# Softmax weights of three head pairs turned as 32x32 squares by VectorE and SBUF copies, in place of TensorE transposes

## The chip, the cores and the metric

The kernel runs on one core of one Trainium2 chip. The metric is the device time of one execution in microseconds (us), lower is better; for the kernel before it is the median of three runs. All durations below come from one profiled execution of that kernel.

## What is computed

One layer of a bidirectional encoder on 512 positions of width 1024 in float32: a recurrent branch and an attention branch side by side, an output projection, a squared-ReLU MLP, norms between. The change is in the attention branch, and in the order of the steps around it:

```
h = RMSNorm(x);  xr, gate, q, k, v = split(h @ W_in)
y_rnn  = (scan_fwd(conv(xr)) + scan_bwd(conv(xr))) * gelu(gate)
y_attn = 8 heads of 64: three windows of dilated keys (128,1),(512,4),(2048,16),
         relative bias, the three outputs combined by their softmax denominators
x = x + concat(RMSNorm(y_rnn), RMSNorm(y_attn)) @ W_out
x = x + relu(RMSNorm(x) @ W_up)^2 @ W_down;  out = RMSNorm(x)
```

The combination of the three windows equals one softmax over the union of the keys, with the logarithm of how often a key occurs added to its logit. The kernel computes it so: one matrix of weights for each head, already with the bias.

## The kernel before

Positions are sorted by parity, so that the 512 positions are four blocks of 128: two of even and two of odd ones. Every matrix product that matters is made of three passes in the fast float format (high times high, high times low, low times high parts, `mm3`); ScalarE makes the high part of a weight (`conv_hi`, tile `whi`), VectorE the low part (`conv_lo`, tile `wlo`), three chunks ahead of TensorE.

The attention stage is one written-out loop, which sets the order on all engines (nothing is reordered): steps `i` = 0..4 and, in each, `u` = 0..3. The heads go in four pairs `p`. A step (i, u) with i < 4 works on pair i and on one block of 128 queries; block numbers follow `QSEQ` = 0, 3, 1, 2. It holds:

- `att_s` (u = 0 and 2, for two u at once): 12 products q times k into `ps`, four PSUM buffers.
- `att_e`: for each of the two heads VectorE adds the bias table `tw` to `ps` and takes the minimum (tile `e`, 128 queries by 416 keys), and ScalarE takes the exponential in place and sums it into `zs`.
- `att_t` and `att_c` (i >= 1, for pair i-1, whose queries are all done): the weights have queries on partitions; the product with `v` wants keys there. For each block of 128 keys and each head, TensorE transposes three 128x128 blocks through PSUM (tile `pt`), ScalarE copies them to `ett`, and VectorE turns the fourth block, of which only 32 columns are used, itself.
- `att_av`: product of `ett` with `v` into `pav`, 12 products for a pair (each is two instructions, as float32 matmuls are in the trace), then VectorE multiplies by `zrow`, the reciprocals of the sums (tile `yp`), and ScalarE squares (`ysq`) and scales it (`at`). Pair 0 is done at (2, 2), before `att_s`; pairs 1 and 2 at (4, 0); pair 3 after the loop.
- `att_z`, `att_zd`: the sums go out to memory (`zd`) at u = 0, and come back spread over the partitions (`zrow`) at u = 2, through SP's queue.
- `load_tw`: four loads of the bias tables at u = 0 and at u = 2, through SP's queue too.
- `fill`: one to four pieces of independent work (`pqk`: projections of the next pairs' q and k; `pwo`: output projection of the recurrent branch), each one `mm3` of three passes, so that TensorE has work while the other engines do the softmax. `FILL` gives their number.
- `beside`: small steps of the recurrent branch, splits of q and k (`s_hi`, `s_lo`), and so on, by the table `plan`.

VectorE, ScalarE and TensorE each take their instructions strictly in this order. SP issues nearly all loads, also in order, and an issue that waits holds up those behind it. Tiles of one 128x512 size come from a ring of 45 (`g_`). Names in the trace: `ps` logits, `e` weights, `ett` turned weights, `pav` product with v, `nbd` bias table in memory, `kk` key parts, `hs` and `ga` recurrent state, `wraw` weights as loaded.

Of the kernel before, what the change touches and what calls it, by code (L numbers as in the profile page):

```python
# [12 lines left out]
FT = mybir.dt.float32  # L13
# [85 lines left out]
def hybrid_kernel(ctx: ExitStack, tc, xw0, xw, xn, w_in, w_v, w_out, w_up, w_dn, gates, vecs, bias, fg, out):  # L99
# [228 lines left out]
    xwt, w3 = [], []  # L328
# [18 lines left out]
    def cvx(k):  # L347
        x, w = xwt[k][:, :S], xwt[k][:, S if k else XG:]
        g = ag[:, k:k + 1] if k else xwt[0][:, S:S + 1]
        hi, lo = g_("w3h", FR), g_("w3l", FR)  # L350
# [143 lines left out]
    def conv_a(t, pp):  # L494
        xr = g_("xr")
        nc.vector.tensor_tensor(in_turn(xr), by_parity(pp), by_parity(rstd), op=OP.mult)
        c = g_("xc")
        act(c, xr, AF.Identity, scale=vec("w2", t), bias=vec("cb", t))
        xrt[t], xc[t] = xr, c

    def conv_b(t):
        xr, c = xrt.pop(t), xc[t]
        stt(c[:, 2:], xr[:, :S - 2], vec("w0", t), c[:, 2:], op0=OP.mult, op1=OP.add)
        stt(c[:, 1:], xr[:, :S - 1], vec("w1", t), c[:, 1:], op0=OP.mult, op1=OP.add)
        stt(c[:, :S - 1], xr[:, 1:], vec("w3", t), c[:, :S - 1], op0=OP.mult, op1=OP.add)
        xcs[t] = swapped("xcs", c)
# [3 lines left out]
    xcs = {}  # L510

    def swapped(name, t):
        o = g_(name)
        for b in range(2):
            nc.sync.dma_start(o[halves[1 - b]], t[halves[b]])
        return o
# [23 lines left out]
    lru_a, lru_t = {}, {}  # L540

    def lru_exp(t):
        for d in range(2):
            r = gact[t, 2 * d]
            a = g_("la")
# [11 lines left out]
    def scan_ops(t):  # L557
# [27 lines left out]
        def keep_hs():  # L585
            r1()
            hs[1] = swapped("hs", hs[1])
            scanned[t] = hs
# [219 lines left out]
    def att_e(p, u):  # L808
# [8 lines left out]
        for e in range(2):  # L817
            h = 2 * p + e
            t = g_("e")
# [9 lines left out]


# [6 lines left out]
    def att_t(h, jt):  # L837
# [5 lines left out]
        t = et[h, jt] = g_("ett")  # L843
# [88 lines left out]

    def att_av(p, jts):
        if 0 in jts:
            pav[p] = ps_("pav", "gs" if p else "pj")
        for jt in jts:
# [193 lines left out]
    for key, fs in (((4, 1, 2), [(att_a, 2), (o_sum, "s1", 0), (o_sum, "s2", 0), (o_sum, "s3", 0), (o_sum, "s3", 1), (o_sum, "22", 0)]),  # L1130
                    ((4, 2, 0), [(o_hi, "s2", 0), (o_hi, "11", 0)]), ((4, 2, 2), [(o_lo, "s2", 0), (o_lo, "11", 0)]),
                    ((4, 3, 0), [(att_q, 2), (o_hi, "11", 1), (o_hi, "s3", 0), (o_hi, "s3", 1)]), ((4, 3, 2), [(o_lo, "11", 1), (o_lo, "s3", 0)]),
                    ((4, 3, 4), [(att_y, 2), (o_lo, "s3", 1), (o_hi2, 0), (o_hi, "s1", 0), (o_hi, "22", 0)])):
        plan[key] = [op(*a) for a in fs]
# [3 lines left out]
    AVS = {(2, 2): (0,), (4, 0): (1, 2)}  # L1138
    with tc.manual_schedule(engines={nc.sync.engine}):
        for i in range(5):  # L1140
            for u in range(4):
                if i < 4:
                    if i == 2 and u == 2:
                        att_av(0, range(4))
                    if u % 2 == 0:
                        att_s(i, (u, u + 1))
                    if u == 2 and i < 3 or u == 0 and i:
                        for e in range(2):
                            load_tw(2 * (i + u // 2) + e, u // 2)
                if i >= 1:  # L1150
# [4 lines left out]
                if i >= 1:  # L1155
# [4 lines left out]
                for p in AVS.get((i, u), ()) if i == 4 else ():  # L1160
                    att_av(p, range(4))
# [4 lines left out]
                if u == (1 if i == 4 else 2) and i >= 1:  # L1166
                    att_zd(i - 1)
# [6 lines left out]
                fill(FILL.get((i, u), (1, 1, 1, 1))[3])  # L1174
                add_x()
# [24 lines left out]
    def wo_x(w, tt):  # L1200
# [3 lines left out]
        if w in ("s4", "21", "s1", "22"):  # L1204
            x1n[g, n] = g_("x1n")
# [75 lines left out]
    rb, opa, opsplit, opdone = {}, {}, {}, set()  # L1281
# [4 lines left out]
    def up_pair(q):  # L1286
# [5 lines left out]
        for n in ("s1", "s2", "s3", "22"):  # L1292
            opa[n, p] = g_("as")
# [64 lines left out]
    def h_hi(n, m):  # L1358
        hsp[n, m] = (g_("hh", FR), g_("hl", FR))
# [155 lines left out]
    for half in range(2):  # L1515
        c0, cd = cu.get((half, 0)), cd_[half]
        rb_done.clear()
        opdone.clear()
        seq = chunks[cd:cd + 7 * NQ]
# [290 lines left out]
```

## Time and profile before

| | |
|---|---|
| median of 3 runs | 525.26 us (525.24 to 526.14) |
| span of the profiled execution | 524.0 us |
| mean DMA rate over the span | 201 GB/s |
| HBM read and written | 95.59 MB and 4.29 MB |
| attention loop, from the first `ps` to the end of the second `pav` group | 94.0 to 165.25 us |

The page gives no other time of the profiled execution than its span. The difference between 525.26 and 524.0 is the start and end that the span leaves out, and the spread of runs.

How to read it: PE is TensorE (PEld its weight loads), DVE VectorE, ACT ScalarE, POOL GpSimd, SP SyncE, SPq and POOLq the DMA queues that they issue to. A row of the timeline is start, duration, engine, line, operation, out<-in with partitions x elements, and in brackets the idle time before it with what ended it. Instructions of one engine overlap a little, so that the distance from start to start is less than a duration. The chain of waits lists the work that ended last, each piece with the time in which nothing else could have ended the program sooner.

### The profile page before, as it was taken

How to read it: one execution, taken by the hardware profiler on the slowest of the kernel's cores; microseconds unless marked ns; L12 is line 12 of the kernel's file. 1: busy time of each engine (PE TensorE's matmuls, PEld its weight loads, DVE VectorE, ACT ScalarE, POOL GpSimd, SP SyncE). 2: the span in 40 equal slices, each digit the busy share in tenths (PEclk: the TensorE clock that was granted, in tenths of full speed). 3: DMA queues.
4: the chain of work that ended last, by engine and by line, in shares of the span. 5: the costliest groups of instructions: out<-in, count | busy, mean ns of one | idle time of the engine just before them, and what ended most of it. 6: DMA issues, size and time to landing. Idle time of an engine off the chain costs nothing.

```text
span 524.0 us, 8211 instructions
## 1 busy us (share of the span) xinstructions
PE 517.3 (99%) x3021; PEld 444.0 (85%) x3021; DVE 430.3 (82%) x668; ACT 351.9 (67%) x568; POOL 65.8 (13%) x90
## 2 busy tenths in 40 slices
PE   9999999999999999999999999999999999999995
PEld 8867888778787788899999888889999999888884
DVE  6899986788886898898789987789766978986985
ACT  7579946667855848585578666565667577655664
POOL 0173000000000321001300311001101300140000
PEclk9999999999999999999999999999999999999999
DMA  8636545367696499847595899976977497799804
GB/s 288 213 98 198 160 155 180 91 182 206 185 286 218 102 194 275 326 129 196 136 225 144 217 273 275 309 268 161 295 235 194 116 226 208 154 286 256 201 1 161
DMA packets 40329, 105.15 MB, mean 201 GB/s; under 512 B 5056, under 2 KB 13376, under 8 KB 40288
## 3 DMA queue, kind: packets, MB, share of 16 engines
q1 hardware_dynamic: 32448, 78.10, 44.7%
q0 software_dynamic: 7696, 26.32, 27.1%
q8 instruction: 24, 0.39, 0.3%
q10 hardware_dynamic: 144, 0.20, 0.1%
q14 instruction: 17, 0.14, 0.1%
HBM read 95.59 MB, written 4.29 MB: 191 GB/s over the span
## 4 chain that ended last, share of the span: by engine, by line
PE 96%; issue 2%; DVE 1%; POOL 1%; DVEq 0%; ACT 0%; POOLq 0%; ACTq 0%
PE pu L313 10%; PE pu L312 10%; PE pu L314 10%; PE pd L312 10%; PE pd L313 10%; PE pd L314 10%; PE pqk L312 3%; PE pqk L314 3%; PE pqk L313 3%; PE pwo L312 2%; PE pt L842 2%; PE pwo L314 2%; PE pwo L313 2%; PE ps L806 2%; PE pav L942 2%
## 5 line engine op out<-in xcount | busy, mean ns | idle before, releaser
L269 DVE TENSOR_TENSOR wlo<-wraw,whi 128x1024 fp32r<-128x1024 f32 x71 | 86.6, 1221 | 23.1 <-ACT whi L247 22.9
L247 ACT ACTIVATE whi<-wraw 128x1024 fp32r<-128x1024 f32 x67 | 70.8, 1058 | 37.5 <-PE pd L314 18.2
L313 PE MATMUL pd<-wlo,ah 128*128 128x512 f32 (+1 forms) x195 | 75.2, 386 | 0.0
L312 PE MATMUL pd<-whi,ah 128*128 128x512 f32 (+1 forms) x195 | 75.2, 386 | 0.0
L314 PE MATMUL pd<-whi,al 128*128 128x512 f32 (+1 forms) x195 | 75.2, 386 | 0.0
L314 PE MATMUL pu<-hh,wlo 128*128 128x256 f32 x224 | 63.4, 283 | 0.0
L313 PE MATMUL pu<-hl,whi 128*128 128x256 f32 x224 | 63.4, 283 | 0.0
L312 PE MATMUL pu<-hh,whi 128*128 128x256 f32 x224 | 63.4, 283 | 0.0
L269 DVE TENSOR_TENSOR wlo<-tw,whi 128x1024 fp32r<-128x1024 f32 x37 | 45.2, 1221 | 18.1 <-ACT whi L247 18.1
L312 PE MATMUL pu<-h2h,whi 128*128 128x256 f32 (+1 forms) x200 | 60.1, 300 | 0.0
L313 PE MATMUL pu<-h2l,whi 128*128 128x256 f32 (+1 forms) x200 | 60.0, 300 | 0.0
L314 PE MATMUL pu<-h2h,wlo 128*128 128x256 f32 (+1 forms) x200 | 60.0, 300 | 0.0
L247 ACT ACTIVATE whi<-tw 128x1024 fp32r<-128x1024 f32 x38 | 40.1, 1059 | 26.3 <-PE pd L314 6.3
L247 ACT ACTIVATE whi<-ts 128x1024 fp32r<-128x1024 f32 x24 | 25.5, 1061 | 26.3 <-PE pd L314 18.3
L312 PEld LDWEIGHTS pu<-hh,whi 128*128 128x128 f32 x224 | 43.0, 192 | 0.0
L313 PEld LDWEIGHTS pu<-hl,whi 128*128 128x128 f32 x224 | 43.0, 192 | 0.0
L314 PEld LDWEIGHTS pu<-hh,wlo 128*128 128x128 f32 x224 | 43.0, 192 | 0.0
L314 PEld LDWEIGHTS pd<-whi,al 128*128 128x128 f32 x195 | 36.6, 188 | 7.4
L312 PEld LDWEIGHTS pd<-whi,ah 128*128 128x128 f32 x195 | 36.6, 188 | 7.3
L313 PEld LDWEIGHTS pd<-wlo,ah 128*128 128x128 f32 x195 | 36.6, 188 | 7.3
L312 PEld LDWEIGHTS pu<-h2h,whi 128*128 128x128 f32 x200 | 38.3, 191 | 1.3
L314 PEld LDWEIGHTS pu<-h2h,wlo 128*128 128x128 f32 x200 | 38.3, 191 | 1.3
(277 smaller groups left out, 1219.8 us busy)
## 6 DMA issues: line engine op xcount, KB each, us to landing
wraw<-in_w_up_dram SPq DMA_DIRECT2D x25, 512.0 KB, 4.4
ts<-in_w_dn_dram POOLq DMA_DIRECT2D x24, 512.0 KB, 13.3
wraw<-in_w_dn_dram SPq DMA_DIRECT2D x24, 512.0 KB, 9.2
tw<-in_w_up_dram SPq DMA_DIRECT2D x15, 512.0 KB, 5.1
tw<-in_w_up_dram POOLq DMA_DIRECT2D x15, 512.0 KB, 8.3
wraw<-in_w_in_dram SPq DMA_DIRECT2D x13, 512.0 KB, 3.8
ts<-in_w_dn_dram SPq DMA_DIRECT2D x8, 512.0 KB, 6.8
tw<-in_w_dn_dram SPq DMA_DIRECT2D x8, 512.0 KB, 7.3
```

What stands on the lines that cost most here:

```text
L247: act(hi, raws[i], AF.Copy)
L269: nc.vector.tensor_tensor(lo, r, f(splits[i][0]), op=OP.subtract)
L312: nc.tensor.matmul(o, lhsT=a[0], rhs=b[0], start=bool(first), stop=False, skip_group_check=on)
L313: nc.tensor.matmul(o, lhsT=a[0], rhs=b[1], start=False, stop=False, skip_group_check=on)
L314: nc.tensor.matmul(o, lhsT=a[1], rhs=b[0], start=False, stop=bool(last), skip_group_check=on)
L806: nc.tensor.matmul(psq[p, u][e][:, :NK], lhsT=qs_[p, a][r, P * qt:P * qt + P], rhs=kks[p][r, b, w:w + NK], start=i == 0, stop=i == 2)
L842: nc.tensor.transpose(pt[:, i * P:(i + 1) * P], en[h][qt][:, k:k + P], ident)
L942: nc.tensor.matmul(pav[p][a, co], lhsT=vs[:, jt, h * DH:(h + 1) * DH], rhs=et[h, jt][:, ci], start=jt == 0 and i == 0, stop=jt == 3 and i ...
```

## The change

For pairs 0, 1 and 2 the turning leaves TensorE and ScalarE. The weights of the two heads of one query block now stand side by side in a tile of 1024 columns (`ez`, two of them, whose unused columns are zero). VectorE turns such a tile in 32x32 squares with one instruction of 128x1024 (`att_d`, tile `turn`, four for a pair). Each 32x32 square is then right in itself, but the squares of a column must still change partitions: 16 copies inside SBUF of 32 partitions by 4 KB each (`att_m`, 128 KB each, 2.1 MB a pair) bring group i of 32 partitions to place j, 11 through SP's queue and 5 through POOL's. `att_av` then reads runs of 32 or 64 columns (`ev_parts`): three products instead of one or two for a key block, with the same sum of 416 columns. It comes at (1, 2), (2, 2) and (3, 2) for pairs 0, 1 and 2, behind `att_s` and ahead of `att_e`. `zrow` is fetched at u = 1. Pair 3 keeps the old way. The ring of 45 tiles becomes a ring of 25, two boxes of eight tiles, two twins of two and one of three; the output projection's steps in `plan` come one or two u earlier.

```diff
-    NG = 45
+    NG = 25
+    def box(name, dt=FT):
+        return work.tile([P, 8, S], dt, name=name, tag="g8", bufs=2)
+    def twin(name):
+        return work.tile([P, 2, S], FT, name=name, tag="g2", bufs=2)
...
     def att_e(p, u):
-            t = g_("e")
+            t = ez[far][:, e, :] if p < 3 or u < 2 else g_("e")
...
+    ez = [twin("e") for _ in range(2)]
+    POS = (0, 2, 3, 1)
+    def att_d(p, u):
+        if u == 0:
+            turn[p] = box("turn")
+        qt = QSEQ[u]
+        nc.vector.transpose(at_(turn[p], P // 4 * POS[qt], [P, 8], [1024, 4], [1, 32]), ez[QT[qt][1]])
+    def att_m(p):
+        t, b = turn.pop(p), box("ett")
+        t, b = [x.rearrange("p (a c) n -> p a (c n)", c=2) for x in (t, b)]
+        for i in range(4):
+            for j in range(4):
+                (nc.gpsimd if 4 * i + j in (3, 6, 9, 12, 15) else nc.sync).dma_start(b[32 * j:32 * j + 32, i, :], t[32 * i:32 * i + 32, j, :])
+        eb[p] = b
...
+    def ev_parts(p, e, jt):
...
+            if jt not in qs:
+                yield at_(b, c, [1024, 4], [1, 64]), at_(o, P * qs[0], [32, 4], [d, 2], [1, 32])
+            else:
+                a0 = 3 * h0
+                yield at_(b, c + 1024 * a0, [1, 64]), at_(o, P * qs[0] + 32 * a0, [d, 2], [1, 32])
+                k = 1 - qs.index(jt)
+                a1 = 1 - h0
+                yield at_(b, c + 1024 * a1 + 32 * k, [1024, 3], [1, 32]), at_(o, P * qs[k] + 32 * a1, [1, 96])
...
-    AVS = {(2, 2): (0,), (4, 0): (1, 2)}
+    AVS = {(1, 2): (0,), (2, 2): (1,), (3, 2): (2,)}
...
-                    if i == 2 and u == 2:
-                        att_av(0, range(4))
                     if u % 2 == 0:
                         att_s(i, (u, u + 1))
+                    for p in AVS.get((i, u), ()):
+                        att_av(p, range(4))
...
-                if i >= 1:
+                if i == 4:
                     att_t(2 * i - 2, u)
                     att_t(2 * i - 1, u)
...
-                if u == (1 if i == 4 else 2) and i >= 1:
+                if u == 1 and i >= 1:
                     att_zd(i - 1)
...
+                if i < 3 and u:
+                    for v in {1: (0, 1), 2: (2,), 3: (3,)}[u]:
+                        att_d(i, v)
+                    if u == 3:
+                        att_m(i)
                 add_x()
```

On TensorE, at step (1, 2), before:

```order
L806 MATMUL ps<-kk,qh 128x416 x8
L806 MATMUL ps<-kk,ql 128x416 x4
L842 MATMUL pt<-ident,e 128x128 x6
L312 MATMUL pqk<-h_hi,whi 128x512
L313 MATMUL pqk<-h_lo,whi 128x512
L314 MATMUL pqk<-h_hi,wlo 128x512
```

and now, the first rows at the same place (shapes are those of the output; nine more rows of `pav` follow, then `pqk`):

```order
L817 MATMUL ps<-kk,qh 128x416 x8
L817 MATMUL ps<-kk,ql 128x416 x4
L992 MATMUL pav<-ett,vs 64x2x32 x2
L992 MATMUL pav<-ett,vs 64x96 x2
L992 MATMUL pav<-ett,vs 64x4x2x32 x4
```

The six transposes are gone, and the product of pair 0 with v, which stood one i later, comes directly behind the logits of pair 1.

On VectorE, from the end of step (1, 1) to the middle of (1, 2), before (`ISA e,mn` and `ISA mn` are the two instructions of the bias sum with its minimum, for one head):

```order
L269 TENSOR_TENSOR wlo<-wraw,whi 128x1024
L615 TENSOR_TENSOR ysq<-ysq 128x512
L822 ISA e,mn<-ps,tw 128x416
L822 ISA mn 128x1
L822 ISA e,mn<-ps,tw 128x416
L822 ISA mn 128x1
L851 STREAM_TRANSPOSE ett<-e 128x32 x2
L765 TENSOR_TENSOR kraw<-pqk,rrow 128x512
```

and now:

```order
L275 TENSOR_TENSOR wlo<-wraw,whi 128x1024
L855 STREAM_TRANSPOSE turn<-e 128x8x4x32 x2
L626 TENSOR_TENSOR ysq<-ysq 128x512
L1007 TENSOR_TENSOR yp<-pav,zrow 128x512
L833 ISA e,mn<-ps,tw 128x416
L833 ISA mn 128x1
L833 ISA e,mn<-ps,tw 128x416
L833 ISA mn 128x1
L776 TENSOR_TENSOR kraw<-pqk,rrow 128x512
L855 STREAM_TRANSPOSE turn<-e 128x8x4x32
```

Two large transposes of pair 1 stand ahead of `yp` of pair 0, which itself stands ahead of the logits of (1, 2); a third follows.

On SP's queue, from the end of step i = 0 into i = 1, before:

```order
L785 DMA kk<-kk 128x2x256
L230 DMA wraw<-in_w_out_dram 128x1024
L476 DMA tw<-nbd 128x384
L478 DMA tw<-nbd 128x2x160
L476 DMA tw<-nbd 128x384
L478 DMA tw<-nbd 128x2x160
L874 DMA zd<-zt 4x32x32
L230 DMA wraw<-in_w_out_dram 128x1024
```

and now:

```order
L796 DMA kk<-kk 128x2x256
L236 DMA wraw<-in_w_out_dram 128x1024
L862 DMA ett<-turn 32x1024 x11
L484 DMA tw<-nbd 128x384
L486 DMA tw<-nbd 128x2x160
L484 DMA tw<-nbd 128x384
L486 DMA tw<-nbd 128x2x160
L910 DMA zd<-zt 4x32x32
L915 DMA zrow<-zd 64x1x512 x2
L236 DMA wraw<-in_w_out_dram 128x1024
```

Eleven of the sixteen copies stand ahead of the bias tables, `zd` and `zrow`; the latter have moved from u = 2 to u = 1.

More of the change, by code (lines that the diff above doesn't have):

```diff
@@ L1204, in wo_x @@
         if w in ("s4", "21", "s1", "22"):
-            x1n[g, n] = g_("x1n")
+            if n == 0 and tt == 0:
+                st["x1n"] = twin("x1n")
+            if w == "s1" and tt == 0:
+                st["x1k"] = work.tile([P, 3, S], FT, name="x1n", tag="kk", bufs=1)
+            x1n[g, n] = st["x1n"][:, tt, :] if n == 0 else g_("x1n") if g == 1 else st["x1k"][:, g and g - 1, :]
         stt(x1n.get((g, n), x1[g, n]), po[b][tt], (nrc if n else rc[1])[:, g:g + 1], x1[g, n], op0=OP.mult, op1=OP.add)
@@ L1291, in up_pair @@
             q = p + HF // 4
-        for n in ("s1", "s2", "s3", "22"):
-            opa[n, p] = g_("as")
+        if not opb:
+            opb.append(box("as"))
+        for n, m in enumerate(("s1", "s2", "s3", "22")):
+            opa[m, p] = opb[0][:, 4 * n + p, :] if n < 2 else g_("as")
         a11, a21, a12, a22 = rb[p, 0], rb.pop((p, 1)), rb[q, 0], rb[q, 1]
@@ L1518, in hybrid_kernel @@
         opdone.clear()
+        opb.clear()
         seq = chunks[cd:cd + 7 * NQ]
```

69 lines of the change are left out of this document (48 added, 21 removed).

## The prediction

> **What bounds the kernel now.** I read the page first: the busy shares, then the chain of work that ended last.
>
> ```profile
> span 524.0 us, 8211 instructions
> PE 517.3 (99%) x3021; PEld 444.0 (85%) x3021; DVE 430.3 (82%) x668; ACT 351.9 (67%) x568; POOL 65.8 (13%) x90
> ...
> PE 96%; issue 2%; DVE 1%; POOL 1%; DVEq 0%; ACT 0%; POOLq 0%; ACTq 0%
> ```
>
> TensorE is busy for 99% of the span and is 96% of the chain, so anything taken off TensorE counts, as long as nothing else becomes late. Next come the busy times by step of the attention loop (rows: i = 0, 1, 2, 3).
>
> ```profile
> 94.00:108.00 14.00, 14.00 (x73) 10.94 (x72) 12.04 (x27) 9.57 (x22) 0.00 (x0) 1.00 0.47 129
> 108.00:124.60 16.60, 16.60 (x97) 13.39 (x96) 12.43 (x37) 12.35 (x30) 0.00 (x0) 1.00 0.64 190
> 124.60:144.20 19.60, 19.60 (x123) 15.01 (x122) 17.50 (x47) 15.20 (x35) 1.04 (x1) 1.00 0.67 184
> 144.20:159.50 15.30, 15.30 (x96) 12.47 (x97) 11.61 (x33) 10.08 (x26) 0.00 (x0) 1.00 0.96 298
> ```
>
> The columns are length, busy PE, PEld, DVE, ACT, POOL, granted clock (1.00 in all four rows), DMA share and GB/s. PE is full in each. VectorE has only 1.96, 4.17 and 2.1 us left in i = 0, 1, 2, and to these the change gives more work.
>
> **What goes from TensorE.** The chain of waits, in order of time, prices a group of six transposes (`pt`), with and without it:
>
> ```profile
> 94.07 1.33 PE ps L806 x12
> 95.40 0.43 PE pqk L312
> ...
> 108.11 1.33 PE ps L806 x12
> 109.44 0.80 PE pt L842 x6
> 110.24 0.23 PE pqk L312
> ...
> 112.75 0.23 PE pqk L314
> 112.98 0.66 PE pt L842 x6
> 113.64 0.23 PE pqk L312
> ...
> 116.41 1.32 PE ps L806 x12
> ...
> 158.83 0.66 PE pt L842 x6
> 159.49 5.76 PE pav L942 x48
> 165.25 0.43 PE pwo L312
> ```
>
> At odd u a group costs 0.66. Behind `ps` it costs 0.80 + 0.23 - 0.43 = 0.60. Twelve groups go: 6 x 0.66 + 6 x 0.60 = **7.56 us**. ScalarE loses 24 copies to `ett`, which nothing waits for once the transposes are gone; I give that nothing.
>
> The product with v keeps its columns, but has 48 instructions a pair where it had 24.
>
> ```profile
> L942 PE MATMUL pav<-ett,vs x96: 299/379/563, 132.9 to 174.0; 128*64 128x416 f32 x32, 128*64 128x256 f32 x32, 128*64 128x160 f32 x32
> 132.93 3.02 PE L942 MATMUL pav<-ett,vs 128*64 128x416 f32 x24
> 136.28 0.68 DVE L948 TENSOR_TENSOR yp<-pav,zrow 128x512 f32<-128x512 f32 x1
> ```
>
> From 160 to 256 columns a duration grows by 80 ns, 0.83 ns a column. The 24 instructions of a pair hold 24 x 277 columns, 5.5 us one after another; the group took 3.02, so the two heads run side by side and columns fill 2.77 of it. Bounds for twice the instructions: 0, or another 3.0 a pair. I take 0.2, since the remainder beyond the columns is 0.25. From the group's start to `yp` are 3.35 us, 3.55 with this.
>
> **What comes to VectorE.** Rows of its timeline in i = 0, and two tile rows of transposes:
>
> ```profile
> 101.15 1.22 DVE L269 TENSOR_TENSOR wlo<-wraw,whi 128x1024 fp32r<-128x1024 f32 x1
> 102.28 0.58 DVE L822 CUSTOM_DVE_ANT_0 e<-ps,tw 128x416 f32<-128x416 f32 x1
> ...
> 104.04 0.69 DVE L765 TENSOR_TENSOR kraw<-pqk,rrow 128x512 f32<-128x512 f32 x1 [0.65 <-PE pqk L314]
> ...
> 105.25 0.58 DVE L822 CUSTOM_DVE_ANT_0 e<-ps,tw 128x416 f32<-128x416 f32 x1
> ...
> 106.27 0.69 DVE L784 TENSOR_TENSOR kk<-kraw,kk 128x512 fp32r<-128x512 f32 x1
> 106.87 1.22 DVE L269 TENSOR_TENSOR wlo<-wraw,whi 128x1024 fp32r<-128x1024 f32 x1
> ...
> L440 DVE STREAM_TRANSPOSE cst<-ysq x2: 702/708/714, 130.2 to 177.6; 128x512 f32<-128x512 f32 x2
> L851 DVE STREAM_TRANSPOSE ett<-e x32: 168/188/208, 110.3 to 170.9; 128x32 f32<-128x32 f32 x32
> ```
>
> Start to start, a pair of logits takes 1.02, a 128x512 operation 0.60, a `wlo` 1.13. Transposes of 32 and 512 columns take 0.188 and 0.708, so 1024 columns make 1.26, or 1.17 start to start. Four a pair are **4.7 us**. In i = 0 the old work ends at 106.87 + 1.13 = 108.00; add 4.7, less the 0.65 of waiting that fills up: the last transpose of pair 0 ends at 112.05. The split `kk` moves from 106.27 to about 109.1 and ends near 109.7, while `att_s` wants it at 108.4: TensorE loses 1.15 there. It reaches the product with v at 116.41 - 1.26 + 1.15 + 1.33 = 117.6, so the copies have 5.5 us.
>
> **What the copies take.** The nearest copies inside SBUF are `xcs`, 128 KB over 64 partitions; then two stretches (the first while two such copies ran, the second with the fastest loads):
>
> ```profile
> L515 SPq DMA_DIRECT2D xcs<-xc x8: 461/568/588, 29.5 to 38.5; - x8
> ...
> DMA to landing us min/median/max: 2.2/2.2/2.4
> ...
> 30.70:31.30 0.60, 0.60 (x4) 0.49 (x3) 0.59 (x1) 0.60 (x2) 0.52 (x2) 1.00 0.95 205
> ...
> 151.00:159.00 8.00, 8.00 (x50) 6.60 (x49) 4.81 (x16) 5.35 (x14) 0.00 (x0) 1.00 0.97 337
> ```
>
> The first lands 2.2 us after its issue. Each further 131 KB takes 0.64 at 205 GB/s, 0.39 at 337, with the DMA engines 95 and 97% busy. Sixteen land 2.2 + 15 x 0.64 = 11.8, or 2.2 + 15 x 0.39 = 8.0 us after the last transpose; issue at 0.57 each on SP is no slower. I take the middle, **9.9**, because part of the time the two queues serve different halves of the partitions.
>
> [...]
>
> **The cycle.** The added wait stands ahead of all TensorE work of (1, 2); behind it `yp`, and in VectorE's order `yp` stands ahead of the next logits, hence of the next pair's transposes. So: last transpose, copies 9.9, product to `yp` 3.55, then VectorE to its next last transpose. For that stretch ScalarE counts too:
>
> ```profile
> 137.05 0.63 ACT L609 ACTIVATE ysq<-yp 128x512 f32<-128x512 f32 x1 [1.79 <-DVE yp L948]
> 137.59 0.71 ACT L962 ACTIVATE at<-yp,vt 128x512 f32<-128x512 f32 x1
> ...
> 138.95 0.64 ACT L823 ACTIVATE e<-e,mn 128x416 f32<-128x416 f32 x1
> ...
> 140.24 0.64 ACT L778 ACTIVATE kk<-kraw 128x512 fp32r<-128x512 f32 x1
> ```
>
> `ysq` 0.54, `at` 0.62, two exponentials 1.29. In i = 1 the third transpose starts 0.77 + 0.54 + 0.62 + 1.29 = 3.2 to 3.3 after `yp`; then 1.17, logits 1.02, `kk` 0.6, a `ysq` that waits for ScalarE till 7.1, 0.6, `wlo` 1.13, transpose 1.17: 10.0. In i = 2: 3.5 + 1.17 + 1.02 + 0.6 + 1.13 + 0.66 + 1.17 = 9.25.
>
> Product of pair 0 at 112.05 + 9.9 = 121.95. Second last transpose 121.95 + 3.55 + 10.0 = 135.5, product of pair 1 at 145.4. Third 145.4 + 3.55 + 9.25 = 158.2, product of pair 2 at 168.1. Then the product itself 3.15 and seven pieces of `pwo` at 0.69, to 176.1; the last exponentials of pair 3 come at about 177.1 (behind `yp` 0.6, two pairs of logits, 0.66 and 1.13, then 1.0 on ScalarE), and the six `pt` end at 177.75. Before, this point was 165.25. So **+12.5 us**: 7.56 saved, and some 20 of new waiting (4.4 at pair 0, about 6 each at pairs 1 and 2, the rest at `kk`, `pt` and the 0.6 of the products). Behind this point the program is the same. The smaller ring and the new boxes I give nothing: the number of tiles is the same, and the one box that waits (`turn`, for the copies of the pair before) is free at 121.95, ahead of `yp`. POOL is idle there but for one 1.04 us instruction.
>
> The span gives 524.0 + 12.5 = 536.5. The median of the runs shown lies 525.26 - 524.0 = 1.26 above the span: **537.8 us**. With 8.0 and 11.8 for the copies, three times -1.9 and +1.9: 532.1 to 543.5.
>
> **Rivals.**
> - *Faster: the copies hide.* If they land within the 5.5 us that TensorE leaves and a transpose of 1024 columns takes 0.5 us or less, so that four fit in the 2 us that VectorE has free, only the gain stays: 525.3 - 7.56 + 0.6 = 518.3. For it: PE is the chain. Against it: 0.708 already for 512 columns, and 2.2 for one copy. Chance 0.15; within 0.2%, between this and the next, 0.05.
> - *VectorE alone sets the pace.* The copies hide, but from one last transpose to `yp` VectorE has, in i = 1, two pairs of logits 2.04, `rz` and `zt` 0.65, six 128x512 operations 3.8, `wlo` 1.13, two transposes 2.34 and `ysq` 0.6, together 10.6, then the 10.0; in i = 2, with the two `yl` and the column sums in place of four of the six, 11.8 and 9.25: last transposes at 112.05, 132.7, 153.7, the third product at 159.2, 168.8 instead of 165.25: 528.8. Chance 0.17.
> - *`zrow` is later than the product.* SP issues it behind eleven copies and four tables, and only once `zd` has landed.
>
> ```profile
> L879 SPq DMA_DIRECT2D zrow<-zd x8: 536/586/876, 120.3 to 165.2; - x8
> ...
> DMA to landing us min/median/max: 3.1/4.9/6.0
> ```
>
>   If the queue is strictly in order, four tables 2.6 behind 9.9, `zd` 0.5, the second issue 0.6 and 3.1 make 16.7 against 13.45: 3.3 for each of pairs 0 and 1, and up to 7.5 for pair 2, behind `ws` and `x`: 544 to 552. No landing of `zd` is in the trace, so I take 0 in the sum and keep this for the range. Chance 0.18.
> - *32 partitions carry half of what 64 do*: 1.28 a copy, 21.4 for sixteen, 572. Chance 0.03. [...]
>
> **How the numbers follow.** Forecast 0.42, `zrow` 0.18, VectorE alone 0.17, hidden 0.15, same 0.05, half rate 0.03. The range 525 to 552 leaves out the hidden case, the half rate and part of the same. About 0.2% is what a measurement of this kernel can tell from no change. Faster 0.15, same 0.05, slower 0.80.
>
> **What would show it.** `pt` x24; TensorE idle ahead of three `pav` groups, with a DMA as releaser, some 4 to 6 us each; a transpose near 1.26 us; `turn` copies landing some 10 us after the last transpose; `yp` 3.5 us behind the start of `pav` (later, if `zrow` rules). No idle ahead of `pav`, or transposes near 0.6, would prove me wrong.

## The result and the profile after

The changed kernel takes 562.36 us (median of four runs, 560.72 to 562.56), the kernel before 525.48 in the same session (525.24 to 526.14): a ratio of 1.069, 95% interval 1.0673 to 1.0707, slower by 37 us. The forecast was 537.8 with a range of 525 to 552: the sign was right, the time lies above the range.

From the page of the changed kernel: span, busy time by engine, and the chain that ended last by engine.

```profile
span 558.7 us, 8300 instructions
PE 523.2 (94%) x3021; PEld 444.8 (80%) x3021; DVE 441.6 (79%) x656; ACT 342.8 (61%) x544; POOL 73.7 (13%) x107
...
PE 60%; DVE 3%; SPq 2%; issue 2%; DMA 2%; POOL 1%; ACT 0%; DVEq 0%; ACTq 0%; POOLq 0%
```

TensorE was busy 99% and is now 94%. Its busy time did not fall by the 7.6 us of the saved transposes; it rose by 6. The same stretches as before the prediction (length, busy PE, PEld, DVE, ACT, POOL, granted clock, DMA share, GB/s):

```profile
94.00:108.00 14.00, 14.00 (x74) 10.90 (x73) 12.81 (x25) 8.21 (x18) 0.00 (x0) 1.00 0.43 127
108.00:124.60 16.60, 10.41 (x60) 7.64 (x60) 12.51 (x25) 6.18 (x15) 2.50 (x5) 0.91 0.76 193
124.60:144.20 19.60, 18.06 (x100) 13.11 (x96) 13.39 (x28) 8.44 (x19) 2.42 (x5) 0.90 0.56 159
144.20:159.50 15.30, 9.16 (x69) 6.72 (x70) 8.09 (x18) 4.16 (x8) 1.05 (x1) 0.78 0.74 187
```

TensorE is no longer full from 108 on, and the granted clock, 1.00 in all four rows before, falls as far as 0.78. VectorE is not full either. The loss is waiting. Here is where: TensorE's timeline at the three products with v (start, duration, instruction, in brackets the idle time ahead of it and what ended it).

```profile
123.10 5.77 PE L992 MATMUL pav<-ett,vs 128*64 128x64 f32 x48 [5.41 <-DMA ett<-turn]
152.00 5.01 PE L992 MATMUL pav<-ett,vs 128*64 128x64 f32 x48 [3.46 <-DMA ett<-turn]
180.39 6.04 PE L992 MATMUL pav<-ett,vs 128*64 128x64 f32 x48 [6.03 <-DMA ett<-turn]
```

And VectorE's timeline at the first transposes of the next pair and at `yp`:

```profile
123.48 2.37 DVE L855 STREAM_TRANSPOSE turn<-e 128x1024 f32<-128x1024 f32 x2 [3.86 <-DMA ett<-turn]
130.70 0.69 DVE L1007 TENSOR_TENSOR yp<-pav,zrow 128x512 f32<-128x512 f32 x1 [4.27 <-DMA zrow<-zd]
...
159.51 0.69 DVE L1007 TENSOR_TENSOR yp<-pav,zrow 128x512 f32<-128x512 f32 x1 [4.23 <-DMA zrow<-zd]
...
190.62 0.69 DVE L1007 TENSOR_TENSOR yp<-pav,zrow 128x512 f32<-128x512 f32 x1 [7.46 <-DMA zrow<-zd]
```

Three things stand out. The idle time ahead of each product, 3.5 to 6 us, is what the prediction expected. The product itself takes 5 to 6 us and not 3.15. And `yp` waits for `zrow`, not for the product. Two windows (columns as above) show the first product and the copies ahead of it:

```profile
112.00:123.00 11.00, 5.69 (x32) 4.31 (x30) 7.50 (x17) 4.82 (x11) 2.50 (x5) 0.94 0.91 239
123.10:128.40 5.30, 5.30 (x46) 4.12 (x48) 2.94 (x3) 0.00 (x0) 0.00 (x0) 0.50 0.58 126
```

While the copies run, the DMA engines are 91% busy at 239 GB/s; the product then runs at a granted clock of 0.50 (the second, 152.00 to 157.01, at 0.62; the third, 180.39 to 186.43, at 0.50). SP's own timeline over the same stretch shows why `zrow` is late:

```profile
111.92 9.15 SPq L862 DMA_DIRECT2D ett<-turn  x11
121.11 0.58 SPq L484 DMA_DIRECT2D tw<-nbd  x1
121.73 0.45 SPq L486 DMA_DIRECT2D tw<-nbd  x1
122.23 0.47 SPq L484 DMA_DIRECT2D tw<-nbd  x1
122.74 0.43 SPq L486 DMA_DIRECT2D tw<-nbd  x1
123.27 0.67 SPq L910 DMA_DIRECT2D zd<-zt  x1
127.50 1.23 SPq L915 DMA_DIRECT2D zrow<-zd  x2
```

`zt` was ready at 113.64 (VectorE's timeline has it from 113.43 for 0.21), but SP issues in order: eleven copies, four tables, then `zd` at 123.27. SP then stands still until `zd` has landed (127.50) and only then issues `zrow`: three such waits, 10.8 us in all, 3.9 the longest.

The chain from the first last transpose to the common point after pair 2, beside the prediction's terms. The measured columns are differences of starts in the trace (last transposes end at 111.90, 140.62 and 169.23; the first `pt` group of the last pair ends at 197.61).

| term | predicted | measured, pairs 0, 1, 2 | later by |
|---|---|---|---|
| end of the first last transpose | 112.05 | 111.90 | -0.15 |
| last transpose to start of product | 9.9 | 11.20, 11.38, 11.16 | 4.04 |
| start of product to `yp` | 3.55 | 7.60, 7.51, 10.23 | 14.69 |
| `yp` to next last transpose | 10.0, 9.25 | 9.92, 9.72 | 0.39 |
| third `yp` to end of the first `pt` group | 6.10 | 6.99 | 0.89 |
| behind that point | 358.75 | 361.09 | 2.34 |

The sum is 22.2, which is 558.7 less the forecast span of 536.5. (The median lies 24.6 over its forecast: the profiled execution, 560.72, was the fastest of the four, and it took 2.0 more than its span where 1.26 had been added.)

Of the 14.69, the product alone accounts for 6.2: it ended 5.8, 5.0 and 6.0 after its start, where `yp` had been forecast for 3.55. The other 8.5 are `zrow`, which came 1.8, 2.5 and 4.2 after the product's end.

### The profile page after: what moved, and what is told of

It is laid out like the page before. It is cut to its first block, busy times and chain, and to the rows that moved or that the text cites. A ratio compares the mean times of both kernels' runs of the same rounds, so it can differ in the third digit from the quotient of the medians.

```text
span 558.7 us, 8300 instructions
## 1 busy us (share of the span) xinstructions
PE 523.2 (94%) x3021; PEld 444.8 (80%) x3021; DVE 441.6 (79%) x656; ACT 342.8 (61%) x544; POOL 73.7 (13%) x107
## 4 chain that ended last, share of the span: by engine, by line
PE 60%; DVE 3%; SPq 2%; issue 2%; DMA 2%; POOL 1%; ACT 0%; DVEq 0%; ACTq 0%; POOLq 0%
PE pu L320 10%; PE pu L319 10%; PE pu L318 10%; PE pd L319 9%; PE pd L318 9%; PE pd L320 9%; SPq L862 1%; DMA zd<-zt 1%; PE pwo L318 1%; PE pwo L320 1%; PE pwo L319 1%; PE pxt L1283 1%; DMA zrow<-zd 1%; POOL wlo L265 0%; DVE e L833 0%
## 5 line engine op out<-in xcount | busy, mean ns | idle before, releaser
L834 ACT ACTIVATE e<-e,mn 128x416 f32<-128x416 f32 x32 | 20.3, 635 | 38.1 <-DVE mn L833 38.1
L319 PEld LDWEIGHTS pu<-h2l,whi 128*128 128x128 f32 x200 | 38.3, 191 | 1.3
```

Of the source, the lines that this page charges most:

```text
L319: nc.tensor.matmul(o, lhsT=a[0], rhs=b[1], start=False, stop=False, skip_group_check=on)
L834: act(x, x, AF.Exp, scale=-1.0, bias=mn, accum_out=zs[p][:, 4 * e + qt:4 * e + qt + 1])
```

## The experiments

All ratios are against the kernel before, run beside each kernel (its medians lie between 525.3 and 525.9). Starting points are the changed kernel (562.36) or an experiment named.

**Whether the copies are the loss.** They are left out, once for all pairs and once for pairs 1 and 2; the products then read the turned tile as it is, with its blocks not exchanged.

```diff
     def att_m(p):
+        eb[p] = turn.pop(p)
+        return
```

> The 48 copies are left out, and the products read the turned tiles in place, so their blocks are not exchanged and what the attention branch gives is another thing; the VectorE transposes stay, with all else. Theory (the copies, and the wait for zrow that they put off, are the loss): TensorE does not idle ahead of the products, the clock stays at 1.0 and the products take 3.1 us; what is left is VectorE's added work, less the transposes saved on TensorE: 523 to 533. Rival (VectorE's transposes are most of the loss): 545 or more.

`e4_nocopy` measured: 533.89 us, 1.0159 (1.0144 to 1.0174): 28.5 us of the 37 go with the copies, and with most of the wait for `zrow`, which they put off. The products took 3.07 each, with no idle time ahead; only the third `yp` still waited, 4.67 for `zrow`.

> Copies for pair 0 alone; the products of pairs 1 and 2 read the turned tiles in place (blocks not exchanged there). Theory (each pair's copies lengthen the way from one last transpose to the next, here by 28.7 - 20.8 = 7.9 us): some 8 us more than e4_nocopy, 540 to 543. Rival (the loss comes from pair 2 alone, where the copies meet the loads of ws and x): 533 to 535.

`e17_pair0` measured: 542.85 us, 1.0322 (1.0295 to 1.0348): 9.0 more than without copies, and three times that is 27. So pair 0 pays about a third of the 28.5, and the last pair alone is not the loss; how pairs 1 and 2 divide the other 19.5 is not shown.

**What is left without copies.** As without copies, and `yp` multiplies by `rstd`, a row that is long there.

```diff
-            nc.vector.tensor_tensor(y[:, ::-1], pav.pop(p), zrow.pop(p), op=OP.mult)
+            z = zrow.pop(p)
+            nc.vector.tensor_tensor(y[:, ::-1], pav.pop(p), z if p == 3 else rstd, op=OP.mult)
```

> The copies are left out as in e4_nocopy, and yp of pairs 0 to 2 multiplies by a row that is long there in place of zrow, so the weights' sums are left out too; zd and zrow are still transferred, in the old order, and nothing waits for them. Theory (VectorE's own work, with nothing waited for, is the floor of this change): yp of pair 2 no longer waits its 4.7 us, and unlike e6_nocopy_zq and e11_nocopy_order no table comes later for it: 528 to 531, slower than before the change all the same. Rival (the floor lies under the kernel before, and order and waits alone made it slow): 518 to 524.

`e14_nocopy_noz` measured: 532.07 us, 1.0126 (1.011 to 1.0143), 1 us over the expected stretch. VectorE's timeline, second and third last transpose:

```profile
131.51 1.24 DVE L855 STREAM_TRANSPOSE turn<-e 128x1024 f32<-128x1024 f32 x1
...
153.35 1.23 DVE L855 STREAM_TRANSPOSE turn<-e 128x1024 f32<-128x1024 f32 x1
```

They end at 132.75 and 154.58; the rival "VectorE alone sets the pace" had 132.7 and 153.7. So that rival was worked out well. With neither copies nor `zrow` waited for, the change is still 6.2 us slower than the kernel before in the same session, although one of its products took 4.04, where the first took 3.08.

Two other ways to get there, with `zd` and `zrow` issued elsewhere, went the other way:

> The 48 copies are left out and the products read the turned tiles in place (blocks not exchanged, another attention result), and zd and zrow of pairs 0 to 2 go out on the POOL queue. Left of the change are VectorE's transposes and the transposes saved on TensorE. Theory (VectorE's own work is then the only thing that sets the pace): the 4.7 us that the third yp waited for zrow in the run without copies go, and the end comes 3 to 5 us earlier: 529 to 531. Rival (TensorE, no longer waiting for copies, sets the pace, and the gain on it shows): 518 to 522. Rival (zrow did not matter once the copies are gone): 534.

`e6_nocopy_zq` measured: 540.13 us, 1.0277: slower than with `zrow` in its old place. VectorE's timeline, third `yp`:

```profile
170.63 0.69 DVE L1009 TENSOR_TENSOR yp<-pav,zrow 128x512 f32<-128x512 f32 x1 [7.67 <-DMA zrow<-zd]
```

The expectation missed that SP's standing still for `zd` also held back tables and weights. On POOL's queue `zd` no longer holds them back: for pair 2 SP issued `ws`, four tables and six loads of `x` between 155.02 and 162.12, `zd` went out among them at 159.33, and `zrow` could be issued only at 167.27, 7.9 us later. Without copies and with `zd` on SP (`e4_nocopy`) that step took 2.5.

> The copies left out as in e4_nocopy (products read the turned tiles in place), and zd and zrow ahead of the tables on SP. Theory (with copies and zrow out of the way VectorE's own work sets the pace, last transposes some 21 us apart; e6_nocopy_zq failed to show it because its tables, no longer held back behind SP's wait for zd, landed ahead of zrow): yp of pair 2 no longer waits its 4.7 us, 528 to 531. Rival (something else, such as the pt groups or the ScalarE copies of the last pair, sets the end): 533 to 534 as in e4_nocopy.

`e11_nocopy_order` measured: 537.68 us, 1.0235. Here `zrow` came in time and the tables late instead:

```profile
166.11 0.59 DVE L833 CUSTOM_DVE_ANT_0 e<-ps,tw 128x416 f32<-128x416 f32 x1 [2.14 <-DMA tw<-nbd]
```

**Moving one wait at a time, with all copies.**

```diff
-        nc.sync.dma_start(bass.AP(tensor=zd.tensor, offset=zd.offset + 32 * P * p, ap=[[32, 4], [P, 32], [1, 32]]), zt)
+        (nc.sync if p == 3 else nc.gpsimd).dma_start(bass.AP(tensor=zd.tensor, offset=zd.offset + 32 * P * p, ap=[[32, 4], [P, 32], [1, 32]]), zt)
```

(and the same for the two `zrow` transfers)

> zd and the two zrow transfers of pairs 0 to 2 go out on the POOL queue, right behind its five copies, and not on SP behind eleven copies and four tables; nothing else is moved. Theory (two things end side by side ahead of each yp, the product at half clock and, a little later, zrow): yp then waits for the product only, 128.9, 157.0 and 186.4 in the trace of the changed kernel where zrow came at 130.6, 159.4 and 190.5, so 1.7 + 2.4 + 4.1 = 8.2 us go: 554. Rival (zrow alone sets the pace): the whole idle time ahead of the three yp goes, 4.3 + 4.2 + 7.5 = 16 us: 546. Rival (VectorE's own work sets the pace, the waits are slack): no change, 562.

`e1_zq` measured: 555.56 us, 1.056 (1.0542 to 1.0577): 6.8 less, near the theory's 8.2. `yp` is now released by the product, but the copies took 13.7, 13.3 and 11.7 where they had taken 11.2. That the number came so near the theory is partly luck: in the two traces the third `yp` is only 3.4 us earlier (187.20 against 190.62), and the spans differ by 2.6; the rest of the 6.8 lies between executions, and no trace shows it.

> Nothing is left out and no queue is changed; on SP zd goes out behind the fifth copy (zt is ready by then) and the two zrow behind the eleventh, ahead of the four tables, where both stood behind the tables. Theory (what makes zrow late is the tables' bytes ahead of zd on the DMA engines and SP's wait for zd; not the queue as such): zrow lands before the product ends, so yp waits for the product alone, and the copies keep their 11 us, where e1_zq, which let tables and weights start earlier, stretched them to 13.5. That is 1.7 + 2.4 + 4.1 us less than the changed kernel: 552 to 555, and up to 3 us less if the later tables also help the copies. Rival (zd and zrow, wherever issued, land behind all that is under way): yp still waits for zrow, 560 to 563.

`e10_order` measured: 555.91 us, 1.0576 (1.056 to 1.0592), just above the theory's 552 to 555. `yp` waited for the product alone, as expected, but VectorE's logits waited for the tables that had been put behind `zrow` (1.20 in pair 1), and the copies took 11.5 to 12.9.

```diff
-    AVS = {(1, 2): (0,), (2, 2): (1,), (3, 2): (2,)}
+    AVS = {(1, 3): (0,), (2, 3): (1,), (3, 3): (2,)}
```

> The product of pair p and its yp stand one step later, at (p+1, 3); zd and zrow stay where they are. Theory (the cycle of copies, product, yp, next transposes): TensorE has a step's more work while the copies run, so its idle ahead of the products falls from 5.4, 3.5 and 6.0 to 3 or less; and VectorE does two pairs of logits and a transpose, some 3 to 5 us, in the time in which it waited for yp, so the next pair's last transpose comes that much earlier, for pairs 1 and 2: 6 to 10 us less, 552 to 556. zrow still keeps yp waiting. Rival (VectorE's own work sets the pace): no change, 562.

`e2_late` measured: 556.36 us, 1.0592 (1.0575 to 1.0609), at the small end of the expectation. TensorE idled 2.97, 0 and 3.77 ahead of the products, which took 3.40, 3.07 and 5.69. VectorE's first transposes of the next pair waited 4.38 for the tile that the copies still read, where they had waited 3.86: that wait did not shrink.

> As e10_order, and the products one step later, at (p+1, 3), as in e2_late: all that the experiments found movable, with nothing left out. Theory: the copies' 11 us and VectorE's next transposes, which wait for them, then set the pace, 24 us from last transpose to last transpose where the changed kernel has 28.7 and the run without copies 21: 545 to 551, still slower than before the change. Rival (the waits overlap so that moving them gains nothing further): 553 to 556 as e1_zq and e2_late each.

`e13_order_late` measured: 557.9 us, 1.061 (1.0592 to 1.0628): the theory failed. Both edits together gave no more than either alone. In the trace the tables, later again, held up the logits of pair 3 by 6.16; that this is the whole reason is not shown.

**The wait for the copies against their mere presence.** The copies run, the product reads the turned tile and waits for none of them.

```diff
     def att_m(p):
+        eb0 = turn[p]
...
-        eb[p] = b
+        eb[p] = eb0
```

> All 48 copies run as in the changed kernel, but the products read the turned tiles in place and wait for no copy (blocks not exchanged in what they use). It tells the wait for the copies from the mere load that they put on the DMA engines and on VectorE's next transposes, which still wait until the copies have read the tile. Theory (the copies cost in three places: the product's wait and its halved clock, zrow behind them, the next transposes' wait for the tile): TensorE does not idle ahead of the products and they take 3.1 us, but yp still waits for zrow and the next transposes for the copies, so most of the loss stays: 554 to 561. Rival (the product's wait is the loss): 534 to 540, near e4_nocopy.

`e12_ghost` measured: 563.62 us, 1.0731 (1.0708 to 1.0754): nothing gained, above the theory's 554 to 561 too, though TensorE did not wait for a copy and every product took 3.07. VectorE's timeline shows it waiting at the transposes and at `yp` as before:

```profile
124.75 2.37 DVE L855 STREAM_TRANSPOSE turn<-e 128x1024 f32<-128x1024 f32 x2 [4.80 <-DMA ett<-turn]
132.75 0.69 DVE L1008 TENSOR_TENSOR yp<-pav,zrow 128x512 f32<-128x512 f32 x1 [5.06 <-DMA zrow<-zd]
```

So the idle time of TensorE, the plainest sign in the profile of the changed kernel, is not by itself what costs. Next the wait for `zrow` alone, with no transfer moved (the edit of `yp` shown above):

> All copies, tables, zd and zrow run as in the changed kernel, but yp of pairs 0 to 2 multiplies by a row that is long there and so waits for no zrow (the weights' sums are left out). Theory (zrow ends last ahead of yp, the product 1.7, 2.4 and 4.1 us before it): 8 us less, 553 to 556, with yp released by the product. Rival (zrow is the whole of the stretch): 546.

`e15_noz` measured: 554.96 us, 1.0558 (1.0534 to 1.0581): 7.4 less, as the theory had it. Then both together:

> As e12_ghost, all copies run and the products wait for none of them, and as in e15_noz yp waits for no zrow. What the copies can still hold up are VectorE's next two transposes, which must not write the tile before it is read, and the tables and weights issued on SP behind them. Theory (copies hold the branch at several places that end within some 5 us of each other, so that taking away one or two gives little): the transposes wait until the copies end, last transposes come 24 to 25 us apart and not 28.7: 546 to 553. Rival (product and zrow together are the loss): 529 to 535, as with the copies left out.

`e16_ghost_noz` measured: 555.22 us, 1.0562 (1.0546 to 1.0578), 2 us over the theory's stretch and far from the rival. With neither wait left, these are VectorE's longest (us in total, times, longest):

```profile
DVE turn L855 <- DMA tw<-nbd: 8.7, 2, 4.7
DVE tw L1120 <- DMA ws<-in_w_out_dram: 8.5, 1, 8.5
DVE x L1047 <- DMA x<-in_xn_dram: 4.7, 1, 4.7
DVE e L833 <- DMA tw<-nbd: 3.1, 2, 2.0
```

The releaser in the first row is the last transfer to come by the profile; the write to `turn` waits for the copies that read it. All four are transfers that SP issues as copies or behind them.

**What the copies' 11 us consist of.** Half the columns of each copy (the other half of the tile is set to zero); and the same copies as eight and eight on the two queues.

```diff
+        nc.gpsimd.memset(b[:, :, 512:], 0.0)
...
-                (nc.gpsimd if 4 * i + j in (3, 6, 9, 12, 15) else nc.sync).dma_start(b[32 * j:32 * j + 32, i, :], t[32 * i:32 * i + 32, j, :])
+                (nc.gpsimd if 4 * i + j in (3, 6, 9, 12, 15) else nc.sync).dma_start(b[32 * j:32 * j + 32, i, :512], t[32 * i:32 * i + 32, j, :512])
```

> Each of the 48 copies moves half of its columns, 64 KB and not 128; the other half of each exchanged tile is set to zero by POOL, which is idle, so half of the weights are left out. Number and issue of the copies are the same. From the end of the last transpose to the start of the product it took 11.0 us. Theory (the DMA engines' time is the limit, 16 x 131 KB at the 240 GB/s of that stretch): the engines need half, and eleven issues on SP at 0.59 and 2.4 to land are then the limit: 8.5 to 9.5 us, and the time falls by some 5 us or more, to 553 to 558. Rival (the issues on SP are the limit): 10.5 to 11 us, 562.

`e7_half` measured: 555.75 us, 1.0575 (1.0559 to 1.0591); last transpose to product 8.6 in all three pairs, where issue alone gives 11 x 0.59 + 2.4 = 8.9 (an estimate from the changed kernel's copies: median of SP's issues 0.59, shortest from issue to landing 2.4).

```diff
-                (nc.gpsimd if 4 * i + j in (3, 6, 9, 12, 15) else nc.sync).dma_start(b[32 * j:32 * j + 32, i, :], t[32 * i:32 * i + 32, j, :])
+                (nc.gpsimd if (i + j) % 2 else nc.sync).dma_start(b[32 * j:32 * j + 32, i, :], t[32 * i:32 * i + 32, j, :])
```

> The same 48 copies, eight of each sixteen on SP and eight on POOL, where eleven and five stood. Theory (the DMA engines' time is the limit): the copies still take 10.5 to 11.5 us, and the time stays within 2 us of 562. Rival (the issues on SP are the limit): 8 x 0.59 + 2.4 = 7 to 8.5 us, and the time falls to 550 to 555.

`e8_split` measured: 563.99 us, 1.0733 (1.0717 to 1.0749); the copies took 12.2, 12.3 and 11.9, a little over the theory's 10.5 to 11.5. Fewer issues on SP did not help and fewer bytes did: the DMA engines' time is the first limit. With half the bytes the copies were 2.6 us shorter, about where the estimate from SP's issues stands. The window of the eight and eight copies:

```profile
112.00:124.00 12.00, 5.59 (x33) 4.28 (x32) 7.40 (x17) 4.83 (x11) 3.95 (x8) 0.90 0.93 227
```

SP's own rows agree (`e7_half`, then `e8_split`):

```profile
111.60 7.01 SPq L863 DMA_DIRECT2D ett<-turn  x11
...
111.79 9.68 SPq L862 DMA_DIRECT2D ett<-turn  x8
```

Eleven half copies went out in 7.01 us; eight whole ones took 9.68, because four of them took 1.54 to 2.06 each, where most take 0.59. So with the engines over 90% busy (0.93 in the window) SP's issues were drawn out too, and a count of issues at 0.59 was not the price.

**The halved clock.** TensorE multiplies a constant while it would wait.

```diff
+            for _ in range(14):
+                nc.tensor.matmul(pav[p][:, :P], lhsT=one, rhs=one, start=True, stop=True)
```

> As e1_zq, and ahead of each of the three products TensorE runs 14 multiplications of a constant by itself (some 3.3 us at full clock) into the product's own bank, which the product then overwrites. They lie in the time in which TensorE waits for the copies. Theory (the product is long because the clock is halved after the idle stretch): the granted clock stays at 1.0 there, the products take about 3.1 us each and not 5.8, 5.0 and 6.0, and since they end last once zrow is early, 7 to 7.5 us more go than in e1_zq: 546 to 547. Rival (the product is long because of its 48 small pieces or because its reads collide with the transfers): the products stay at 5 to 6 us and the time is that of e1_zq or up to 1 us more.

`e5_zq_warm` measured: 556.22 us, 1.0588 (1.0571 to 1.0605), no different from its starting point. Inconclusive: idle times of 3.57 and 3.65 were left, and only the second product was short (3.5).

> As e1_zq, with 25, 13 and 21 multiplications of a constant ahead of the three products (6.1, 3.1 and 5.1 us at 0.24 each), so that TensorE idles for 2 us or less there, where e5_zq_warm with 14 left 3.6, 0.9 and 3.7 and kept the product short (3.3) in the second pair only. Theory (an idle stretch between 3.0 and 3.5 us or longer halves the clock, and nothing else makes the product long): all three products take 3.1 to 3.4 us with the granted clock at 1.0, the cycle is 2.7 + 1.8 + 2.6 us shorter than in e1_zq, 548 to 550. Rival (the first and third products are long for another reason, such as reads of tiles that transfers still write next to): 5.5 to 6 us there, 554 to 557.

`e9_zq_keep` measured: 555.07 us, 1.0564 (1.0537 to 1.0591). The products took 6.05, 3.42 and 4.7; idle times of 2.90 and 2.51 were left ahead of the first and the third. The granted clock over the first was 0.50 (126.8 to 132.8). The theory's limit of 3.0 to 3.5 us was wrong: 2.90 lies below it.

> As e15_noz (yp waits for no zrow, all transfers as in the changed kernel), and TensorE runs 20, 8 and 22 multiplications of a constant by itself ahead of the three products (4.9, 1.9 and 5.3 us at 0.24 each), so that at most a microsecond of its idle time is left there, where e9_zq_keep left 2.9, 0 and 2.5 and kept only the second product short. In e15_noz yp was released by the product in all three pairs, and the products took 5.8, 6.0 and 5.3. Theory (the product's length at half clock lies on the way): 3.1 to 3.5 each and 4 to 8 us less than e15_noz: 547 to 551. Rival (transfers behind the copies, tables and x, are next in line, and take what the product gives): products short, but 552 to 555.

`e18_noz_keep` measured: 554.27 us, 1.0557 (1.054 to 1.0575). Now all products were short, as TensorE's timeline shows (the third, from 177.54, took 3.5):

```profile
123.54 3.40 PE L994 MATMUL pav<-ett,vs 128*64 128x64 f32 x48 [1.58 <-DMA ett<-turn]
...
148.47 3.40 PE L994 MATMUL pav<-ett,vs 128*64 128x64 f32 x48
```

The granted clock over the first, in a window (third number from the right):

```profile
123.60:127.00 3.40, 3.29 (x49) 2.54 (x50) 2.96 (x4) 0.00 (x0) 0.00 (x0) 1.00 0.72 176
```

So the constant work cured the product, which settles what made it long: the clock (over the first product 1.00 here, 0.50 in the changed kernel), not its 48 pieces. But the time hardly moved (554.96 without it): the rival held. By the second `yp` VectorE was 4.3 us ahead of `e15_noz` (151.91 against 156.22; 0.4 of it from before the first copies), by the third last transpose only 1.6 (ended at 165.94 against 167.57), since the wait for `x` grew from 1.97 to 4.66:

```profile
164.04 0.75 DVE L1048 SCALAR_TENSOR_TENSOR x<-pwo,rcol,x 128x512 f32<-128x512 f32 x1 [4.66 <-DMA x<-in_xn_dram]
```

> As e18_noz_keep, and zd and zrow of pairs 0 to 2, which nothing reads there, are not transferred at all, so SP no longer stands still until zd has landed (123.7 to 127.6, 148.6 to 152.9 in e18_noz_keep) before it issues the tables, ws and x. Theory (with yp and the product out of the way, what SP issues late behind copies and zd is next: VectorE waited 4.66 us for x in e18_noz_keep): x lands some 5 us earlier, that wait goes, and the end comes 4 to 6 us earlier: 548 to 551. Rival (the DMA engines are full and x lands when it did): 553 to 555.

`e19_nozd_keep` measured: 550.54 us, 1.0465 (1.0442 to 1.0489), as the theory had it: the wait for `x` is gone. VectorE's waits that are left (total, times, longest):

```profile
DVE tw L1122 <- DMA ws<-in_w_out_dram: 9.0, 1, 9.0
DVE turn L855 <- DMA ett<-turn: 4.4, 1, 4.4
DVE turn L855 <- DMA tw<-nbd: 3.7, 1, 3.7
DVE e L833 <- DMA tw<-nbd: 3.3, 5, 2.0
```

Together 20.4 us, against the 18.5 that still separate this kernel from the one that waits for neither copies nor `zrow` (532.07). The two numbers are near each other, but a sum of waits is not shown to be the loss. No version that computes everything came below 555 us, so none beats the kernel before.

## Why the prediction was wrong in size

**The account.** From the kernel before, adding: VectorE's transposes and all else but copies and `zrow` 525.5 to 532.1 (+6.6, with the 7.56 saved already in it; the smaller ring, which the prediction gave nothing, is in it too and was not tested by itself); the wait for `zrow` 533.9 (+1.8 without copies, where it is 7.4 with them); copies of pair 0 542.9 (+9.0); copies of pairs 1 and 2 562.4 (+19.5).

**What goes from TensorE, 7.56.** Nothing here contradicts it: `pt` stands at 24 instructions, as foretold. The gain is inside the +6.6 and not seen by itself, since TensorE does not set the pace any more.

**VectorE's transposes, 1.26 each.** Right: 1.24 (median 1.235 of twelve). The first last transpose was forecast for 112.05 and ended at 111.90. `att_s` of pair 1 lost 0.66 to `kk` where 1.15 was forecast.

**The copies, 9.9.** Right in kind, 1.3 too short each: 11.2, 11.4, 11.2. The middle between 8.0 and 11.8 was taken because two queues were hoped to help. No run shows that they do: eleven and five copies took 11.2 to 11.4, eight and eight 11.9 to 12.3, both nearer to 11.8. Other loads shared the engines as well: 239 GB/s over the 11.0 us of the window are 2.6 MB, of which the copies are 2.1.

**Product to `yp`, 3.55. This is the step that failed**: 14.7 of the 22.2 us (7.60, 7.51 and 10.23 for the 3.55 forecast). Two parts of it were wrong.

- `zrow` at "0 in the sum". It was priced as a rival (3.3 for pairs 0 and 1, up to 7.5 for pair 2, chance 0.18), and it came about: 4.05, 3.96 and 6.68 over the sum, as the last of two things to end. The row that gave it away stood in the prediction: 3.1 to 6.0 from issue to landing, behind eleven copies and four tables. Without its wait, 7.4 us went.
- The product at 3.15. The prediction foretold 4.4 to 6 us of idle TensorE ahead of it and priced it at a clock of 1.00 all the same; it ran at 0.53, 0.62 and 0.50 for 5 to 6 us. The gaps ahead of the three products were of 3.46 to 6.03; in `e9_zq_keep` the clock was 0.50 behind one of 2.90 as well, and in `e2_late` 1.00 behind one of 2.97. On the time by itself it did next to nothing here: with the wait for `zrow` gone, three short products gave 0.7 us (554.96 to 554.27), less than the intervals tell apart, because tables and `x` were next.

**One path where there were four.** The cycle (last transpose, copies, product, `yp`, next last transpose) was forecast to the half microsecond where it was worked out: `yp` to the next last transpose took 9.9 and 9.7 against 10.0 and 9.25. But it was taken as the only path out of the copies. The runs show three more beside it, ending within some 5 us of each other: `zd` and `zrow`; VectorE's next two transposes, which must not write `turn` while copies read it (priced at nothing, "free at 121.95, ahead of `yp`"; true, but next in line once `yp` came sooner); and tables, `ws` and `x`, which SP issues behind the copies. That is why taking away the product's wait alone gave nothing, `zrow`'s 7.4, both 7.1, and all copies 28.5.

`e18_noz_keep` is the test of this: there product to `yp` took 3.44, 3.44 and 3.53, as forecast, and the span, 551.7, is still 15.2 over the forecast one. The copies, at 12.0, 11.6 and 11.6, are 5.5 of it; `yp` to the third last transpose, with the wait for `x`, took 14.0 in place of 9.25; 5.8 came behind the third `yp`, and small gains make up the difference. So the failed step was the largest term, but setting it right does not bring the forecast time: what the sum lacked is that other terms too are held up by the copies, or by what SP issues behind them.

**Behind the common point, 2.34.** The prediction called the program there the same. 1.6 of it are two waits on TensorE that were absent before (0.9 for `x`, 0.7 for `ett` of the last pair); the rest stays open.

**The rivals.** "VectorE alone" was the best-worked figure of all, for a kernel that was not built: 528.8 against 532.07, with last transposes right to 0.1 and 0.9 and the point behind the first `pt` group at 168.7, where 168.8 was forecast; most of the 3.3 that it missed came behind that point. "Copies hide" and "32 partitions carry half" fell: 16 copies took 11 us, neither 5.5 nor 21.

What stays open: how the last 18.5 us divide among the writes to `turn`, `ws` and the tables. Whether a third large tile, with which the next transposes need not wait for the copies, would bring the time down stays open too: no run has one.

## What to carry to other kernels

When a change puts a long transfer on an engine's in-order path, list everything that is issued behind it on the same queue and everything that must wait until its source is read, and price each as a path of its own: the loss is set by the last of them, and removing one shows only the next. A tie between two late things ("`zrow` is later than the product") belongs in the sum with the later value, not in a rival. And where a few microseconds of idle time on TensorE are forecast, price the work right behind them at half the clock too: here the product took 5.0 to 6.0 us behind gaps of 3.46 to 6.03 (changed kernel) and 6.05 behind one of 2.90 (`e9_zq_keep`), though 3.40 behind one of 2.97 (`e2_late`).

## What the runs showed of the hardware

- In the trace of the changed kernel, from 90 to 214 us, the granted clock is 0.50 from 121.64 to 128.47, 148.95 to 155.78, 176.26 to 186.50 and 193.32 to 196.74, else 1.00: the halved stretches last 6.83, 6.83, 10.24 and 3.41 us, all multiples of 3.41. Counted in intervals of 3.41 from the first of these, backward and forward, every interval with 1.96 us or more of idle TensorE (1.96, 2.19, 3.05, 3.13, and 3.41 twice) was followed by one at 0.50. So were two with 0.72 and 1.46, themselves at 0.50; behind one with 1.51, itself at 1.00, the clock stayed at 1.00. So idle time by itself does not tell, and neither does the length of a gap: 2.97 us idle (121 to 124 in `e2_late`) left the clock at 1.00, 2.90 us (124 to 127 in `e9_zq_keep`) did not. The rows of the two products:

```profile
123.80:127.10 3.30, 3.19 (x48) 2.44 (x48) 2.94 (x3) 0.00 (x0) 0.00 (x0) 1.00 0.73 174
...
126.80:132.80 6.00, 6.00 (x49) 4.18 (x49) 2.94 (x3) 0.00 (x0) 0.00 (x0) 0.50 0.82 250
```

- On another queue `zd` was not early: on POOL's, without copies (`e6_nocopy_zq`), it was issued at 114.40 and landed at 118.53, right behind four tables that SP had issued before it, the last of which landed at 118.23.
